# One hybrid decoder layer on one core: the first x tile in one transfer, the first weight split between pairs of x blocks, more idle matmuls at the start

## The chip, the core and the metric

The kernel runs on one core of a Trainium2 chip. The core has a matrix engine (PE), a vector engine (DVE), a scalar engine (ACT), a general engine (POOL), a queue engine that issues transfers (SP), and 16 DMA engines that move data between the device memory and the on-chip memory. The engines run side by side, each through its own list of instructions in order, and wait for one another through semaphores. The metric is the device time of one execution in microseconds (us); lower is better. One execution was also taken with the hardware profiler, and all the rows below come from it.

## What is computed

A decoder layer on 256 positions of width 1024, all in float32. Cut to what matters:

```python
h = rms_norm(x, norm_mix_pre)                 # x: (256, 1024)
proj = h @ w_in                               # w_in: (1024, 9232)
qa, ka, va, qd, kd, vd, zd, bd, ad, ga, gd = split(proj)
ya = moba_attention(rope(qa), rope(ka), va)   # block-sparse attention, 8 heads
yd = gated_deltanet(qd, kd, vd, zd, bd, ad)   # conv, chunked delta rule, gated norm
merged = sigmoid(ga) * (ya @ w_o_attn) + sigmoid(gd) * (yd @ w_o_delta)
x = x + rms_norm(merged @ w_out, norm_mix_post)
h = rms_norm(x, norm_ffn_pre)
f = (silu(h @ w_gate) * (h @ w_up)) @ w_down  # inner width 2816
out = x + rms_norm(f, norm_ffn_post)
```

The part that the change touches is the very beginning: x is loaded and transposed, scaled by the columns of norm_mix_pre, and multiplied by the first 414 columns of w_in that are needed, those with bd and ad and the first part of the gates.

## The kernel before

Every float32 product is made from three faster ones. Each operand is split into a rounded high half and a low half (the rest), and PE adds high x high, low x high and high x low in one bank of its result memory. So each weight piece goes through three steps: SP loads it as `wr` (four buffers in turn), ACT copies it rounded to `wh`, DVE subtracts to get `wl`. The pieces are numbered in the order of their use. `split_to` does a whole piece at once; `split_halves` (line 441) does one of the first two in two steps of 414 columns. x comes in two tiles of 128 rows, `q_x` in the trace (x0 and x1 in the code). PE transposes a tile in eight blocks of 128 x 128 into banks, two blocks to a bank and four to a call of `x_transpose` (line 504). `x_evac` (line 510) then splits each block: ACT writes the high half `q_hh`, scaled by a column of `col0`, and DVE the low half `q_hl`. It goes through the four blocks in the order 0, 2, 1, 3, from one bank to the other and back. `col0` holds norm_mix_pre in columns: eight rows are loaded as `rows0` and transposed by PE.

`start` (line 1109) is the first unit. It issues idle matmuls on a zero tile (`fill`, with the counts WARM and FILL), the transposes of x0, again idle matmuls, and then `part(i, t)`, the six matmuls of weight piece i with x tile t. In between stand the transposes of x1 and the splits of the pieces wr1, wr2 and wr3. At its end the row scales of x are worked out: two times a sum of squares on ACT, a power on POOL and a diagonal `d_dg` on DVE, which PE multiplies by ones. From then on every unit has the same form: load, split, multiply.

`K` is a table of constants that SP loads after the first four weight pieces and some small rows. `mask16` (a cast of a part of K on DVE) and `triur` (a copy of a part of it on ACT) are needed only much later. Their lines stand in another function, `gates`; where they end up in the lists of DVE and ACT is decided when the program is built, by a scheduler that goes by its own estimates. SP issues a transfer only when the completion counter that it is to use is free again; there are eight in turn. So SP issues K when the second x tile has landed, the transfer that had the counter before.

Helpers record every operation, so the trace gives one line for many: 132 is the wrapper of ACT, DVE, POOL and SP, 290 a matmul, 294 a transpose and 1121 an idle matmul. Buffer numbers are left out in the trace.

Of the kernel before, what the change touches and what calls it, by code (L numbers as in the profile page):

```python
# [27 lines left out]
PSUM = bass.MemoryType.PSUM  # L28
MARGIN = 50
STAG = 0  # L30
WARM = 5
DEC = 6
KEEP = 1
FILL = 3


def shape_constants():
# [215 lines left out]
def build(nc, tc, ctx, A):  # L253
    fl = Flow()
    SP, ACT, DVE, POOL, PE = nc.sync, nc.scalar, nc.vector, nc.gpsimd, nc.tensor
    SP, ACT, DVE, POOL = Engine(SP, "S", fl), Engine(ACT, "A", fl), Engine(DVE, "V", fl), Engine(POOL, "P", fl)
# [24 lines left out]
    def mm(out, l, r, start, stop):  # L281
        n = free_size(r)
        if l.dtype == F32R:
            c = max(109.0, 0.4225 * n)
        elif l.dtype == F32:
            c = max(213.0, 1.667 * n)
        else:
            c = max(29.0, 0.44 * n)
        fl.pe(out, l, r, c)
        issue(lambda: PE.matmul(out, l, r, start=start, stop=stop))  # L290

    def tr(out, in_, idn):
        fl.pe(out, in_, idn, 107.0)
        issue(lambda: PE.transpose(out, in_, idn))  # L294
# [11 lines left out]
    def main_bank():  # L306
        while not banks.ok():
            yield banks.ok
        return banks.get([128, 512], F32, "m")
# [22 lines left out]
    rows0 = cst.tile([8, 128], F32, name="rows0")  # L332
    col0 = cst.tile([128, 8], F32, name="col0")
# [17 lines left out]
    xd, wind = A["x"][0], A["w_in"][0]  # L351
# [61 lines left out]
    def load_to(i):  # L413
        while nl[0] <= min(i, len(P) - 1):
            j = nl[0]
            ap, a, b = P[j]
            t = wraw.tile([128, a, b], F32, name=f"wr{j}", tag="wr")
            if isinstance(ap, list):
                w = b // len(ap)
                for i, part in enumerate(ap):  # L420
                    SP.dma_start(t[:, :, w * i:w * i + w], part)
            else:
                SP.dma_start(t, ap)
            raws[j] = t
            nl[0] += 1
# [15 lines left out]
    def split_halves(j):  # L441
        load_to(j)
        _, a, b = P[j]
        r = raws.pop(j)
        hi = wsp.tile([128, a, b], F32R, name=f"wh{j}", tag="wh")
        lo = wsp.tile([128, a, b], F32R, name=f"wl{j}", tag="wl")
        for i in range(a):
            ACT.activation(hi[:, i], r[:, i], AF.Copy)
            DVE.tensor_tensor(lo[:, i], r[:, i], hi[:, i].bitcast(F32), op=ALU.subtract)
        spl[j] = (hi, lo)  # L450
        ns_[0] += 1
        load_to(j + RAW)
        return hi, lo

    def piece(j, la=LA):
        split_to(j + la)
        return spl[j]

    xt = []
    for t in range(2):  # L460
        xx = s4.get([128, 1024], F32, f"x{t}")
        if t == 0:
            for q in range(2):
                SP.dma_start(xx[:, 512 * q:512 * q + 512], xd[0:128, 512 * q:512 * q + 512])
                if q == 0:
                    SP.dma_start(rows0, A["norm_mix_pre"].rearrange("o (k p) -> (o k) p", p=128))
            load_to(1)
        else:
            SP.dma_start(xx, xd[128:256, :])
        xt.append(xx)  # L470
    load_to(RAW - 1)
    SP.dma_start(rows[0:96], A["conv_w"][0].rearrange("i (b p) -> (i b) p", p=128))
# [16 lines left out]
    def split_out(bank_ap, hi_ap, lo_ap, scale=None):  # L489
        if scale is None:  # L490
            ACT.activation(hi_ap, bank_ap, AF.Copy)
            DVE.tensor_tensor(lo_ap, bank_ap, hi_ap.bitcast(F32), op=ALU.subtract)
        else:
            ACT.activation(hi_ap, bank_ap, AF.Copy, scale=scale)
            DVE.scalar_tensor_tensor(lo_ap, bank_ap, scale, hi_ap.bitcast(F32), op0=ALU.mult, op1=ALU.subtract)

    def act_slots(tag):
        his, los = [], []
        for q in range(2):
            his.append((yield from slot(s4, [128, 4, 256], F32R, f"{tag}h{q}")))  # L500
            los.append((yield from slot(s4, [128, 4, 256], F32R, f"{tag}l{q}")))
        return his, los

    def x_transpose(src, q):
        bs = [(yield from main_bank()), (yield from main_bank())]
        for i in range(4):
            tr(bs[i // 2][:, 128 * (i % 2):128 * (i % 2) + 128], src[:, 512 * q + 128 * i:512 * q + 128 * i + 128], ident)
        return bs

    def x_evac(bs, cols, t, his, los, q):  # L510
        ts = slice(128 * t, 128 * t + 128)
        for i in (0, 2, 1, 3):
            k = 4 * q + i
            split_out(bs[i // 2][:, 128 * (i % 2):128 * (i % 2) + 128], his[q][:, i, ts], los[q][:, i, ts],
                      scale=cols[:, k:k + 1])
        main_put(bs[0])
        main_put(bs[1])

    def transpose_scaled(src, cols, t, his, los, q):
        x_evac((yield from x_transpose(src, q)), cols, t, his, los, q)  # L520
# [11 lines left out]
    def main_put(b):  # L532
        banks.put(b)
# [453 lines left out]
    def two_banks():  # L987
        b0 = yield from main_bank()
        b1 = yield from main_bank()
        return [b0, b1]  # L990
# [116 lines left out]
    hT = []  # L1107

    def start():
        hT.extend((yield from act_slots("h")))  # L1110
        with tc.manual_schedule():
            warm = cst.tile([128, 512], F16, name="warm")
            DVE.memset(warm, 0.0)
            DVE.memset(mhalf, -0.5)
            DVE.memset(ones, 1.0)
            ACT.activation(scr[:, 0:4], mhalf[:, 0:4], AF.Square)
            wb = yield from main_bank()

            def fill(n):
                for i in range(n):  # L1120
                    PE.matmul(wb, warm[:, 0:128], warm, start=True, stop=True)

            fill(WARM)
            tr(wb[:, 0:8], rows0, ident[0:8, 0:8])
            DVE.tensor_copy(col0, wb[:, 0:8])
            ev = []
            for q in range(2):
                ev.append((yield from x_transpose(xt[0], q)))
            fill(FILL)
            main_put(wb)  # L1130
            outs = yield from two_banks()
            x_evac(ev[0], col0, 0, hT[0], hT[1], 0)
            pc = [split_halves(0)]
            x_evac(ev[1], col0, 0, hT[0], hT[1], 1)
            pc.append(split_halves(1))

            def part(i, t):
                hi, lo = pc[i]
                n = hi.shape[2]
                ts = slice(128 * t, 128 * t + 128)  # L1140
                for kk in range(2):
                    k = 2 * i + kk
                    ah, al = hT[0][k // 4][:, k % 4, ts], hT[1][k // 4][:, k % 4, ts]
                    mm(outs[t][:, :n], ah, hi[:, kk, :], k == 0, False)
                    mm(outs[t][:, :n], al, hi[:, kk, :], False, False)
                    mm(outs[t][:, :n], ah, lo[:, kk, :], False, k == 7)

            part(0, 0)
            e0 = yield from x_transpose(xt[1], 0)
            part(1, 0)  # L1150
            e1 = yield from x_transpose(xt[1], 1)
            x_evac(e0, col0, 1, hT[0], hT[1], 0)
            pc.append(piece(2, 0))
            x_evac(e1, col0, 1, hT[0], hT[1], 1)
            part(0, 1)
            part(1, 1)
            nrs = {}
            for i in range(2):
                pc.append(piece(3, 0)) if i == 0 else None
                part(2 + i, 0)  # L1160
                part(2 + i, 1)
            for t in range(2):
                ss, rs[t], nrs[t] = small(1), small(1), small(1)
                sq = yield from slot(s4, [128, 1024], F32, "sq")
                ACT.activation(sq, xt[t], AF.Square, accum_out=ss)
                s4.put(sq)
                rs_from(ss, 1.0 / D, rs[t])
                DVE.tensor_scalar(nrs[t], rs[t], -1.0, None, op0=ALU.mult)
                split_to(4 + t)
            ACT.activation(ex, abc, AF.Exp)  # L1170
            b = yield from main_bank()
            tr(b[:, 0:105], rows[0:105, :], ident[0:105, 0:105])
            DVE.tensor_copy(colp[:, 0:105], b[:, 0:105])
            main_put(b)
            held.append(DVE.tensor_copy(id16, ident).ins)
        s4.put(xt[0], xt[1])
        for t in range(2):
            ACT.activation(beta[:, 8 * t:8 * t + 8], outs[t][:, 0:8], AF.Exp, scale=nrs[t])
            DVE.scalar_tensor_tensor(tt[:, 8 * t:8 * t + 8], outs[t][:, 8:16], rs[t], dtb, op0=ALU.mult, op1=ALU.add)
        yield from gate_evac(0, outs)  # L1180
        fl.add("gates", gates())
        yield from spread([rs[0], rs[1]], rsb)
# [207 lines left out]
```

## Time and profile before

| | us |
|---|---|
| median of 3 runs | 549.88 (549.68 to 550.12) |
| the profiled execution | 549.29 |
| its span, first to last instruction | 547.6 |
| PE busy | 534.8 (98%) |
| DVE busy | 368.1 (67%) |
| ACT busy | 315.0 (58%) |
| the 16 DMA engines, share of the span | 53% |

The profiled execution has 1.7 us outside its span. A busy PE tells little about how fast it goes: its clock is granted at one of two levels, 1.2 or 2.4 GHz, and the view of stretches gives the mean of it as a share (1.00 is 2.4 GHz). The chain of waits is followed back from the last instruction: at each step to what released it. A transfer in it stands from its issue to its landing. In the timeline a row joins instructions of one kind that follow each other, and the bracket at its end tells how long the engine stood idle before it and what released it.

### The profile page before, as it was taken

To read this page: it belongs to the slowest core of one execution; us is meant where nothing else is said; L and a number is where in the kernel's file an instruction comes from. 1 tells how busy PE (TensorE), PEld (TensorE's weight loads), DVE (VectorE), ACT (ScalarE), POOL (GpSimd) and SP (SyncE) were. 2 spreads that over 40 slices of the span, in tenths; PEclk is the share of its full clock that TensorE was granted. 3 is DMA by queue.
4 is the path that set the end of the run, shared out by engine and by line. 5 is a ranking of instruction groups with operands and counts; after the bars stand their busy time and mean duration, and the time that the engine had idled before them with its cause. 6 is when DMAs were issued, how large, how long until landed. Compare 5 with 4: busy or idle time off the path is not lost.

```text
span 547.6 us, 8378 instructions
## 1 busy us (share of the span) xinstructions
PE 534.8 (98%) x3156; PEld 460.6 (84%) x3156; DVE 368.1 (67%) x650; ACT 315.0 (58%) x553; POOL 26.4 (5%) x38
## 2 busy tenths in 40 slices
PE   7999999899999999999999999999999999999995
PEld 5988898898989888899889988778888888888884
DVE  4899876895879787866577567586465554554434
ACT  6868658487654965786526544585444544443331
POOL 0000002200000230000000000010000000000000
PEclk8999999999999999999999999999999999999998
DMA  8947765245455252244465766257666665555612
GB/s 258 255 149 216 218 197 150 78 117 167 129 168 158 78 167 64 63 148 155 131 201 187 247 210 195 77 158 259 202 189 193 180 197 176 181 189 192 193 38 78
DMA packets 63035, 90.40 MB, mean 165 GB/s; under 512 B 3233, under 2 KB 35090, under 8 KB 62994
## 3 DMA queue, kind: packets, MB, share of 16 engines
q1 hardware_dynamic: 62994, 89.86, 53.4%
q8 instruction: 25, 0.41, 0.3%
q14 instruction: 16, 0.13, 0.1%
HBM read 88.80 MB, written 1.05 MB: 164 GB/s over the span
## 4 chain that ended last, share of the span: by engine, by line
PE 85%; DVE 4%; ACT 3%; DMA 3%; issue 2%; POOL 2%; SPq 0%; POOLq 0%; DVEq 0%; ACTq 0%
PE b_m L290 73%; PE b_s L290 8%; PE b_s L294 2%; PE b_m L294 2%; DMA q_x<-in_x 1%; DVE wl L132 1%; POOL tiny L132 1%; DMA K<-in_shape_k 1%; DMA wr<-in_w_in 1%; ACT wh L132 1%; ACT L132 0%; DVE h_a L132 0%; DVE q_vT L132 0%; SPq L132 0%; ACT d_js L132 0%
## 5 line engine op out<-in xcount | busy, mean ns | idle before, releaser
L132 DVE TENSOR_TENSOR wl<-wr,wh 128x1024 fp32r<-128x1024 f32 (+3 forms) x168 | 197.8, 1184 | 120.8 <-ACT wh L132 116.9
L132 ACT ACTIVATE wh<-wr 128x1024 fp32r<-128x1024 f32 (+3 forms) x168 | 171.8, 1030 | 151.6 <-PE b_m L290 142.9
L290 PE MATMUL b_m<-wh,q_fh 128*128 128x512 f32 x264 | 103.5, 392 | 0.5 <-DVE q_fl L132 0.5
L290 PE MATMUL b_m<-wl,q_fh 128*128 128x512 f32 x264 | 103.0, 390 | 0.0
L290 PE MATMUL b_m<-wh,q_fl 128*128 128x512 f32 x264 | 102.7, 390 | 0.0
L290 PE MATMUL b_m<-wh,q_hh 128*128 128x512 f32 (+2 forms) x208 | 83.1, 400 | 1.0 <-ACT wh L132 1.0
L290 PE MATMUL b_m<-wl,q_hh 128*128 128x512 f32 (+2 forms) x208 | 78.8, 379 | 0.0
L290 PE MATMUL b_m<-wh,q_hl 128*128 128x512 f32 (+2 forms) x208 | 78.8, 379 | 0.0
L290 PEld LDWEIGHTS b_m<-wh,q_fh 128*128 128x128 f32 x264 | 49.6, 188 | 11.0 <-DVE q_fl L132 1.0
L290 PEld LDWEIGHTS b_m<-wl,q_fh 128*128 128x128 f32 x264 | 49.6, 188 | 10.7 <-DVE wl L132 0.7
L290 PEld LDWEIGHTS b_m<-wh,q_fl 128*128 128x128 f32 x264 | 49.5, 188 | 10.3
L290 PE MATMUL b_m<-q_hh,wh 128*128 128x256 f32 x192 | 56.3, 293 | 0.0
L290 PE MATMUL b_m<-q_hl,wh 128*128 128x256 f32 x192 | 54.4, 283 | 0.0
L290 PE MATMUL b_m<-q_hh,wl 128*128 128x256 f32 x192 | 54.4, 283 | 0.0
L290 PEld LDWEIGHTS b_m<-wh,q_hh 128*128 128x128 f32 x208 | 39.5, 190 | 5.4 <-ACT wh L132 1.5
L290 PEld LDWEIGHTS b_m<-wh,q_hl 128*128 128x128 f32 x208 | 39.5, 190 | 5.3
L290 PEld LDWEIGHTS b_m<-wl,q_hh 128*128 128x128 f32 x208 | 39.6, 190 | 4.3 <-DVE wl L132 0.5
L132 POOL TENSOR_TENSOR tiny<-tiny,mhalf 128x4 f32<-128x4 f32 (+1 forms) x20 | 17.4, 873 | 471.3 <-DVE tiny L132 471.3
L290 PEld LDWEIGHTS b_m<-q_hh,wh 128*128 128x128 f32 x192 | 36.7, 191 | 0.4
L290 PEld LDWEIGHTS b_m<-q_hl,wh 128*128 128x128 f32 x192 | 36.7, 191 | 0.3
L290 PEld LDWEIGHTS b_m<-q_hh,wl 128*128 128x128 f32 x192 | 36.7, 191 | 0.1
L132 ACT ACTIVATE h_U<-b_s 128x256 f16<-128x256 f32 (+1 forms) x28 | 11.5, 415 | 10.9 <-PE b_s L290 10.9
(204 smaller groups left out, 718.0 us busy)
## 6 DMA issues: line engine op xcount, KB each, us to landing
wr<-in_w_in SPq DMA_DIRECT2D x56, 512.0 KB, 3.8
wr<-in_w_down SPq DMA_DIRECT2D x22, 512.0 KB, 3.3
wr<-in_w_gate SPq DMA_DIRECT2D x20, 512.0 KB, 3.7
wr<-in_w_up SPq DMA_DIRECT2D x20, 512.0 KB, 3.7
wr<-in_w_in SPq DMA_DIRECT2D x12, 412.0 KB, 3.4
wr<-in_w_o_attn SPq DMA_DIRECT2D x8, 512.0 KB, 4.4
wr<-in_w_o_delta SPq DMA_DIRECT2D x8, 512.0 KB, 4.2
wr<-in_w_out SPq DMA_DIRECT2D x8, 512.0 KB, 3.7
```

What stands on the lines that cost most here:

```text
L132: r = f(*args, **kw)
L290: issue(lambda: PE.matmul(out, l, r, start=start, stop=stop))
L294: issue(lambda: PE.transpose(out, in_, idn))
```

## The change

Four things, all in the first microseconds of the program:

- x0 is loaded by one transfer of 128 rows of 4 KB instead of two of 2 KB rows, and the small transfer of rows0 is issued by ACT instead of SP.
- WARM goes from 5 to 7, FILL from 3 to 8: more idle matmuls ahead of the transposes of x0 and behind them.
- The four blocks of x0's first half are split in the order 0, 1, 2, 3 in two pairs. Weight piece 0 is split behind the first pair and piece 1 behind the second, then come the four blocks of x0's second half.
- `x_evac` gets its order as an argument and frees its banks when the last block is through.

```diff
-WARM = 5
+WARM = 7
-FILL = 3
+FILL = 8
...
+    ACT.dma_start(rows0, A["norm_mix_pre"].rearrange("o (k p) -> (o k) p", p=128))
     xt = []
     for t in range(2):
         xx = s4.get([128, 1024], F32, f"x{t}")
-        if t == 0:
-            for q in range(2):
-                SP.dma_start(xx[:, 512 * q:512 * q + 512], xd[0:128, 512 * q:512 * q + 512])
-                if q == 0:
-                    SP.dma_start(rows0, A["norm_mix_pre"].rearrange("o (k p) -> (o k) p", p=128))
-            load_to(1)
-        else:
-            SP.dma_start(xx, xd[128:256, :])
+        SP.dma_start(xx, xd[128 * t:128 * t + 128, :])
+        load_to(1)
         xt.append(xx)
...
-    def x_evac(bs, cols, t, his, los, q):
+    def x_evac(bs, cols, t, his, los, q, order=(0, 2, 1, 3)):
...
-        for i in (0, 2, 1, 3):
+        for i in order:
...
-        main_put(bs[0])
-        main_put(bs[1])
+        if order[-1] == 3:
+            main_put(bs[0])
+            main_put(bs[1])
...
-            x_evac(ev[0], col0, 0, hT[0], hT[1], 0)
+            x_evac(ev[0], col0, 0, hT[0], hT[1], 0, (0, 1))
             pc = [split_halves(0)]
+            x_evac(ev[0], col0, 0, hT[0], hT[1], 0, (2, 3))
+            pc.append(split_halves(1))
             x_evac(ev[1], col0, 0, hT[0], hT[1], 1)
-            pc.append(split_halves(1))
```

The lists of DVE and ACT change by more than the lines that were moved. This is DVE's list before, from the first split of x blocks to the split of piece 3 (names carry a number; `wl_169`, `wl_185`, `wl_225` and `wl_251` are pieces 0 to 3, an operation on 128x128 is one block of x):

```order
L132 SCALAR_TENSOR_TENSOR q_hl_125<-b_m,col_78,q_hh_124 128x128 x4
L132 TENSOR_TENSOR wl_169<-wr_102,wh_168 128x414 x2
L132 SCALAR_TENSOR_TENSOR q_hl_127<-b_m,col_78,q_hh_126 128x128 x4
L132 TENSOR_TENSOR wl_185<-wr_104,wh_184 128x414 x2
L132 SCALAR_TENSOR_TENSOR q_hl_125<-b_m,col_78,q_hh_124 128x128 x4
L132 CAST mask_76<-K 128x128
L132 TENSOR_TENSOR wl_225<-wr_108,wh_224 128x828
L132 SCALAR_TENSOR_TENSOR q_hl_127<-b_m,col_78,q_hh_126 128x128 x4
L132 TENSOR_TENSOR wl_251<-wr_110,wh_250 128x828
```

And DVE's list after, for the same stretch (`wl_171`, `wl_183`, `wl_231` and `wl_257` are pieces 0 to 3):

```order
L132 SCALAR_TENSOR_TENSOR q_hl_124<-b_m,col_78,q_hh_123 128x128 x2
L132 TENSOR_TENSOR wl_171<-wr_101,wh_170 128x414 x2
L132 SCALAR_TENSOR_TENSOR q_hl_124<-b_m,col_78,q_hh_123 128x128 x2
L132 TENSOR_TENSOR wl_183<-wr_103,wh_182 128x414 x2
L132 SCALAR_TENSOR_TENSOR q_hl_126<-b_m,col_78,q_hh_125 128x128 x4
L132 SCALAR_TENSOR_TENSOR q_hl_124<-b_m,col_78,q_hh_123 128x128 x2
L132 CAST mask_76<-K 128x128
L132 SCALAR_TENSOR_TENSOR q_hl_124<-b_m,col_78,q_hh_123 128x128 x2
L132 TENSOR_TENSOR wl_231<-wr_107,wh_230 128x828
L132 SCALAR_TENSOR_TENSOR q_hl_126<-b_m,col_78,q_hh_125 128x128 x4
L132 TENSOR_TENSOR wl_257<-wr_109,wh_256 128x828
```

One pair of x0's blocks has moved behind piece 0, and the cast of the mask has moved ahead of the last pair of x1's first four blocks. On ACT the list before, from the conversion of piece 1 to that of piece 3 (`wh_184`, `wh_224`, `wh_250`):

```order
L132 ACTIVATE wh_184<-wr_104 128x414 x2
L132 ACTIVATE q_hh_124<-b_m,col_78 128x128 x4
L132 ACTIVATE wh_224<-wr_108 128x828
L132 ACTIVATE q_hh_126<-b_m,col_78 128x128 x2
L132 ACTIVATE triur<-K 128x128
L132 ACTIVATE q_hh_126<-b_m,col_78 128x128 x2
L132 ACTIVATE wh_250<-wr_110 128x828
```

And on ACT after, for the same stretch (`wh_182`, `wh_230`, `wh_256`):

```order
L132 ACTIVATE wh_182<-wr_103 128x414 x2
L132 ACTIVATE q_hh_125<-b_m,col_78 128x128 x4
L132 ACTIVATE q_hh_123<-b_m,col_78 128x128 x2
L132 ACTIVATE triur<-K 128x128
L132 ACTIVATE q_hh_123<-b_m,col_78 128x128 x2
L132 ACTIVATE wh_230<-wr_107 128x828
L132 ACTIVATE q_hh_125<-b_m,col_78 128x128 x4
L132 ACTIVATE wh_256<-wr_109 128x828
```

`triur` has moved ahead of two of x1's first blocks, of the conversion of piece 2 and of two of x1's last blocks.

## Rows read from the trace of the kernel before

**Rows 1.** The page: busy time of PE, share of the span, instructions.

```profile
PE 534.8 (98%) x3156; PEld 460.6 (84%) x3156; DVE 368.1 (67%) x650; ACT 315.0 (58%) x553; POOL 26.4 (5%) x38
```

**Rows 2.** The chain of waits, 0 to 40 us: start us, us, what.

```profile
3.05 6.79 DMA q_x<-in_x
...
9.86 3.99 DMA K<-in_shape_k
...
13.87 0.04 DVE mask L132
...
14.01 1.01 DVE wl L132
...
16.76 1.02 DVE wl L132
...
17.80 0.16 DVE tiny L132
...
21.24 13.89 PE b_m L290 x102
```

**Rows 3.** DMA engines, 0 to 16 us in 40 slices: busy tenths, GB/s.

```profile
DMA  0000378689779999999999999999999697999999
GB/s 0 0 0 0 61 271 302 138 255 210 151 188 265 166 240 327 377 421 415 437 392 400 387 391 393 380 276 290 346 378 380 216 157 165 229 297 276 283 329 347
```

**Rows 4.** Timeline of SP: start us, us, engine line operation out<-in count [idle before].

```profile
1.25 0.36 SPq L132 DMA_DIRECT2D rows<-in_norm_mix_pre  x1
...
2.06 0.94 SPq L132 DMA_DIRECT2D wr<-in_w_in  x2
...
9.86 0.33 SPq L132 DMA_DIRECT2D K<-in_shape_k  x1
```

**Rows 5.** Timeline of DVE, 0 to 24 us.

```profile
8.01 1.09 DVE L132 TENSOR_TENSOR wl<-wr,wh 128x414 fp32r<-128x414 f32 x2 [1.62 <-ACT wh L132]
...
10.49 1.09 DVE L132 TENSOR_TENSOR wl<-wr,wh 128x414 fp32r<-128x414 f32 x2
11.50 0.60 DVE L132 SCALAR_TENSOR_TENSOR q_hl<-b_m,col,q_hh 128x128 fp32r<-128x128 f32 x2
12.28 0.61 DVE L132 SCALAR_TENSOR_TENSOR q_hl<-b_m,col,q_hh 128x128 fp32r<-128x128 f32 x2 [0.18 <-ACT q_hh L132]
```

**Rows 6.** Timeline of ACT, 0 to 24 us.

```profile
7.43 0.99 ACT L132 ACTIVATE wh<-wr 128x414 fp32r<-128x414 f32 x2 [1.42 <-DMA wr<-in_w_in]
...
9.39 0.62 ACT L132 ACTIVATE q_hh<-b_m,col 128x128 fp32r<-128x128 f32 x2 [0.47 <-DVE q_hl L132]
9.92 0.97 ACT L132 ACTIVATE wh<-wr 128x414 fp32r<-128x414 f32 x2
...
12.40 0.89 ACT L132 ACTIVATE wh<-wr 128x828 fp32r<-128x828 f32 x1
...
13.87 0.31 ACT L132 ACTIVATE triur<-K 128x128 fp32r<-128x128 f32 x1
```

**Rows 7.** Timeline of PE, 0 to 24 us.

```profile
1.25 2.31 PE L1121 MATMUL b_m<-warm 128*128 128x512 f16 x5 [1.25 <-DVE mhalf L132]
...
5.71 0.66 PE L294 MATMUL b_m<-ident,q_x 128*128 128x128 f32 x4 [0.89 <-DMA q_x<-in_x]
6.21 0.81 PE L1121 MATMUL b_m<-warm 128*128 128x512 f16 x3
8.03 0.62 PE L290 MATMUL b_m<-wh,q_hh 128*128 128x414 f32 x1 [1.01 <-ACT wh L132]
...
21.24 0.70 PE L290 MATMUL b_m<-d_dg,ones 128*128 128x256 f32 x2 [0.22 <-DVE d_dg L132]
```

**Rows 8.** Stretches: us, busy time (and count) by engine, PE clock, DMA share, GB/s.

```profile
8.03:9.90 1.87, 1.87 (x6) 1.59 (x7) 1.70 (x5) 1.40 (x5) 0.00 (x0) 0.53 1.03 396
9.90:11.40 1.50, 1.50 (x8) 1.36 (x7) 1.41 (x4) 1.44 (x5) 0.00 (x0) 0.50 1.05 308
...
14.00:17.80 3.80, 3.80 (x21) 3.55 (x19) 3.18 (x7) 2.66 (x7) 0.00 (x0) 1.00 1.07 304
```

## The prediction

> **What bounds the kernel now.** I read the page first: PE is busy for 98% of the span [rows 1], so time is won or lost only where PE starts late or stands still. Then the chain of waits over the first 40 us [rows 2], because the change touches nothing behind it: apart from names, the instructions of every engine stand in the same order in both kernels from the split of wr3 on. The reader is to see there that the chain is not on PE until 21.24. It runs over the load of the second x tile, the load of the constants K (issued at 9.86, landed 3.99 later, 13.85), the cast of the mask that waits for it, the splits of weight pieces wr2 (14.01) and wr3 (16.76 to 17.78), the two row-scale chains (from 17.80), and only then 102 matmuls of PE in a row. PE itself waits 0.22 us at 21.24 for DVE's d_dg [rows 7]: from 8 to 21 us PE and the pair ACT/DVE run nearly level, with ACT/DVE last. From 21.24 PE is the chain. So what the change does to the time is how much earlier or later the matmul of 21.24 can start; that shift goes through to the end, since what follows is PE work, or waits for work that starts equally later.
>
> **The change part by part.**
>
> *Transfers.* SP issues x's first tile as one transfer instead of two, and rows0 goes to ACT's queue, so wr0 is issued right behind x, where the second issue stood: at about 1.25 instead of 2.06, 0.8 us earlier [rows 4]. It helps only as far as the DMA engines had room. They show it: from 2.0 to 4.8 us the slices read 7, 8, 6, 8, 9, 7, 7 tenths, from 4.8 on 9 [rows 3]. The gaps add up to 0.4 x (0.3+0.2+0.4+0.2+0.1+0.3+0.3) = 0.7 us, somewhat less since the digits are rounded down. The bytes are the same. I call s the time by which everything behind x lands earlier, and take 0.6. Lower bound 0: the gaps stay, or one engine's queue was full anyway and the last of its packets sets the landing. Upper bound 1.6: the slices from 2.8 to 6.0 carry only 138 to 265 GB/s, about 200 on average, where those from 6.4 on carry 377 to 437 [rows 3]; if that slow stretch of 3.2 us came from the split of x, the same bytes would take 1.6 us. I lean to the gaps, because the slow stretch goes on after x's second half was read at 5.71 [rows 7]. K is issued, before and after, when the second x tile has landed (its completion counter is used again), so K moves with s too: to 13.85 - 0.6 = 13.25.
>
> *x in one piece, seven warm fills.* Two more fills at 2.31 / 5 = 0.46 us each [rows 7] put the transposes, and so the first block of x on ACT, 0.9 us later. Before, ACT was through with four blocks and then waited 1.42 us for wr0 at 7.43 [rows 6]; that wait, and two blocks instead of four, cover the 0.9. It would cost only if s went beyond about 1.
>
> *Weight split behind two blocks.* Before, four blocks of the first quarter were split while wr0 was on its way, for nothing. Now two of them stand behind wr0's split, on both engines. On DVE the way from ACT's start on wr0 (7.43) to the cast was 0.58 to wl0 (8.01), 2.48 to wl1 (10.49), 1.01 to the next pair (11.50), 0.6 for it and 0.8 for the pair at 12.28 [rows 5, 6]. In the new order it is wl0, pair, wl1, four blocks, pair, cast. The moved pair reads one bank, and in this kernel ACT's second block of a bank starts only when DVE is through with the first (ACT stood 0.47 us at 9.39 for that [rows 6]); so it takes about 0.35 + 0.4 + 0.35 us, not 0.6. Summed: 0.58 + 2.48 + 1.01 + 0.6 + about 1.0 = 5.7 us from ACT's start on wr0, so DVE is at the cast at 6.83 + 5.7 = 12.5. K lands at 13.25. The extra work is hidden by the wait for K, with 0.7 us left, and this holds for every s, since both ends move with it. It comes on the path only if K lands more than 0.7 us earlier than wr0's shift makes it.
>
> *What now stands behind K.* This is the term that counts, and the diff doesn't show it; the order does. Cast and triur wait for K, and they have moved up by one pair on DVE and by wr2's conversion and two blocks on ACT. Before, ACT converted wr2 at 12.40 to 13.29, before K was there [rows 6], and DVE could split it at 14.01, 0.16 after K's landing [rows 2]. Now behind K come, on ACT: triur (0.31), a pair of blocks (0.62, as at 9.39), wr2's conversion (0.89), each starting some 0.1 before the one ahead of it ends, as wr1's did at 9.92 behind the pair [rows 6]; that puts the conversion at +0.79 to +1.68, and DVE splits wr2 at +1.70. PE's matmuls with the second x tile wait for the pair, those with wr2 for the split. That is 1.54 later behind K. From there the pattern is the old one: 2.75 us from wr2's split to wr3's (14.01 to 16.76), 1.04 to the row scales (17.80), 3.44 to PE's matmul at 21.24 [rows 2]; the same instructions in the same order. Bounds of this term: 1.2, if the pair behind K overlaps better; 1.9, if it waits block by block. I take 1.54, which is from rows of just these instructions.
>
> *Eight fills.* Three before, eight now, at 0.81 / 3 = 0.27 us [rows 7]: 8 x 0.27 = 2.2 us. The transposes, at 5.71 before for x's second half, are all through by then or a little earlier, so the fills end near 7.7 at most, and wr0's first half is ready at about 7.4 (8.03 - 0.6). A delay of PE of 0.3 at most. They cover the 1.01 us in which PE waited before the first matmul [rows 7]. After that wait the granted clock was 0.53 and 0.50 from 8.03 to 11.40, the lower level, 1.2 GHz [rows 8]; kept at 2.4 GHz the stretch of 3.37 us would need half, 1.7 us. I count this at nothing: PE gets through earlier and then waits for the pair of blocks behind K. Its work that is left then, 33 matmuls of this unit at 3.80 / 21 = 0.18 us [rows 8], is 6 us beside the 8.3 that ACT and DVE take from there to the d_dg matmul, and waits for wr2 and wr3 in between.
>
> The Trainium skill, page "TensorE: Matmul & The Clock Gate", section "What's actually happening", says that "the default state is throttled, and activity releases the throttle". By that rule alone the fills give the stretch its full clock, and the sum would be a gain; the rows agree on the clock, but the chain of waits says that it isn't PE that ends last there.
>
> *Sum.* +1.54 behind K, -0.6 from the earlier landing: the matmul of 21.24 starts at 22.18, 0.94 us later. The profiled execution took 549.29 (span 547.6 and 1.7 around it), so 550.2 by its own measure; the median of the runs, 549.88, lies 0.59 above it, and with it I predict 549.88 + 0.94 = 550.8. A measurement of this kernel can tell about 0.2%, 1.1 us, from no change: the forecast is inside, near its slow end.
>
> **The rivals.**
>
> *Slower: the transfers don't move.* If the last packet of wr0 and of x's second tile comes from an engine whose queue was full from 3.5 us on, s is 0 to 0.4 and the 1.54 stays nearly whole: 551.0 to 551.4. It decides at s = 0.44. For it: from 4.8 us on the digits show no room [rows 3]. Against: the visible gaps ahead of that. A second fall of the clock, while PE stands before the blocks behind K, would add up to 0.5 us: 551.9 at most. 0.33 together.
>
> *No change, lower: the slow stretch goes.* If one transfer of x ends the stretch at 200 GB/s, s is 1.0 to 1.6, K lands at 12.3 to 12.9, and the sum is +0.5 to -0.1: 549.8 to 550.4. For it: the low rate begins with x's second half. Against: it outlasts it. 0.16.
>
> *Faster: PE ends last after all.* If ACT and DVE had more slack than the chain says, the clock kept up gives up to 1.7 us: 548.2. For it: PE had no idle to speak of from 8.03 to 11.40 and from 14.0 to 17.8 [rows 8]. Against: the wait at 21.24, and the pair behind K. 0.10.
>
> That the fills don't bridge the wait (the load later than they last) is a case without a price of its own: the forecast's time.
>
> **How the numbers follow.** Forecast, s from 0.44 to 1.0, 550.4 to 551.0: 0.41. Slower 0.33, the earlier load 0.16, PE last 0.10. Faster by over 0.2% is then 0.10, within it 0.41 + 0.16 = 0.57, slower 0.33. The range runs from 549.5 (the earliest load, less a few tenths of spread: the runs before lie 0.4 apart) to 551.8, and leaves out the faster case and the end of the slow one.
>
> **What would show it.** In the profile of the changed kernel: wr issued at about 1.25; K landed at 13.0 to 13.5; the cast of the mask behind an idle of some tenths on DVE; wr2's conversion on ACT behind triur, not before it; the split of wr2 1.7 us behind K's landing; the d_dg matmul near 22.2 with a wait of PE in front of it; granted clock 1.00 from 8 to 11 us without the end coming nearer. I am wrong if the chain of waits runs over PE between 8 and 21 us, or if K lands before 12.7 or after 13.7.

## The result, and the profile after

The changed kernel takes 552.68 us (median of 4 runs, 552.30 to 552.77) beside 549.78 for the kernel before on the same chip: a ratio of 1.0052, 95% interval 1.0039 to 1.0064, so 2.9 us (2.1 to 3.5) slower. The span of the profiled execution grew from 547.6 to 551.0 us. The forecast was 550.8 and its range ended at 551.8; the time lies 0.9 above it.

PE's share of the span hardly moved; it has seven matmuls more than in [rows 1]. On the page:

```profile
PE 536.1 (97%) x3163; PEld 460.8 (84%) x3163; DVE 368.3 (67%) x650; ACT 314.5 (57%) x553; POOL 26.4 (5%) x38
```

The chain of waits of the changed kernel, 0 to 47 us (start us, us, what), answers to [rows 2]:

```profile
2.21 6.50 DMA q_x<-in_x
8.73 5.69 DMA K<-in_shape_k
...
14.44 0.31 ACT triur L132
14.75 0.51 ACT q_hh L132 x2
15.26 0.79 ACT wh L132
...
16.08 1.02 DVE wl L132
...
18.84 1.02 DVE wl L132
...
23.31 13.89 PE b_m L290 x102
...
40.54 5.14 DMA wr<-in_w_in
...
45.76 0.04 ACT wh L132
```

Two losses can be read off it. The first: the d_dg matmul starts at 23.31 instead of 21.24, 2.07 later. From K's landing to it, it is now 8.89 us (14.42 to 23.31) instead of 7.39 (13.85 to 21.24), because triur, a pair of blocks and wr2's conversion stand ahead of wr2's split; and K itself landed 0.57 later in this execution. The second I had not looked for: at 40.54 the chain passes over a weight transfer of 5.14 us. The same transfer stands in the chain of the kernel before too, but there it took 3.68:

```profile
38.48 3.68 DMA wr<-in_w_in
```

That is 1.46 us more, and 2.07 + 1.46 = 3.5 is the whole growth of the span (3.4). PE's own starts say the same: counted from the end of the program, a matmul at 49 us starts 2.05 later than in the kernel before, one at 55 us 3.52 later, and the last one 3.49.

The stretches of the changed kernel (us, busy time and count by engine PE, PEld, DVE, ACT, POOL, PE clock, DMA share, GB/s) and the first real matmul of PE, beside [rows 7, 8]; and the first instructions of DVE and ACT behind K:

```profile
8.03:9.90 1.87, 1.87 (x12) 1.67 (x11) 1.35 (x4) 1.61 (x5) 0.00 (x0) 1.00 1.05 390
9.90:11.40 1.50, 1.50 (x12) 1.44 (x11) 1.32 (x5) 1.03 (x5) 0.00 (x0) 1.00 1.12 316
11.40:14.00 2.60, 1.07 (x7) 0.57 (x5) 0.64 (x3) 0.25 (x1) 0.00 (x0) 1.00 0.92 236
```

```profile
8.28 0.54 PE L290 MATMUL b_m<-wh,q_hh 128*128 128x414 f32 x1
...
15.06 0.46 PE L290 MATMUL b_m<-wh,q_hh 128*128 128x414 f32 x1 [2.59 <-ACT q_hh L132]
```

```profile
14.44 0.23 DVE L132 CAST mask<-K 128x128 f16<-128x128 f32 x1 [2.40 <-DMA K<-in_shape_k]
```

```profile
14.44 0.31 ACT L132 ACTIVATE triur<-K 128x128 fp32r<-128x128 f32 x1 [2.79 <-DMA K<-in_shape_k]
14.66 0.61 ACT L132 ACTIVATE q_hh<-b_m,col 128x128 fp32r<-128x128 f32 x2
15.16 0.89 ACT L132 ACTIVATE wh<-wr 128x828 fp32r<-128x828 f32 x1
```

The clock reads 1.00 where it read 0.53 and 0.50, and PE does 24 matmuls from 8.03 to 11.40 instead of 14 (transposes and idle ones counted). Nothing comes of it: all three engines then stand before K or what waits for it, ACT for 2.79 us, DVE for 2.40, PE for 2.59.

### The profile page after: what moved, and what is told of

It is laid out like the page before. It is cut to its first block, busy times and chain, and to the rows that moved or that the text cites. A ratio compares the mean times of both kernels' runs of the same rounds, so it can differ in the third digit from the quotient of the medians.

```text
span 551.0 us, 8390 instructions
## 1 busy us (share of the span) xinstructions
PE 536.1 (97%) x3163; PEld 460.8 (84%) x3163; DVE 368.3 (67%) x650; ACT 314.5 (57%) x553; POOL 26.4 (5%) x38
## 4 chain that ended last, share of the span: by engine, by line
PE 85%; DVE 4%; DMA 3%; ACT 3%; issue 2%; POOL 2%; SPq 0%; POOLq 0%; DVEq 0%; ACTq 0%
PE b_m L290 73%; PE b_s L290 8%; PE b_s L294 2%; PE b_m L294 1%; DVE wl L132 1%; DMA q_x<-in_x 1%; POOL tiny L132 1%; DMA K<-in_shape_k 1%; DMA wr<-in_w_in 1%; ACT wh L132 1%; DVE h_a L132 0%; DVE q_vT L132 0%; ACT d_js L132 0%; DVE tiny L132 0%; DVE h_T L132 0%
```

## Why a weight transfer far behind the start became slower

The DMA view of the stretch around that transfer tells it: busy tenths and GB/s in 40 slices, then the queues (packets, MB, share). First before (38.4 to 43.6 us), then after (40.5 to 45.7):

```profile
GB/s 0 0 0 0 0 0 0 0 24 118 110 110 138 217 335 331 343 347 347 351 347 347 335 284 158 106 197 264 280 311 280 284 315 347 347 343 296 213 142 99
q1 hardware_dynamic: 2076, 1.05, 71.0%
```

```profile
GB/s 0 0 0 0 0 0 0 0 150 79 91 87 189 303 307 335 311 339 323 343 323 339 327 288 205 134 173 291 315 311 319 343 319 335 339 307 272 118 59 55
...
q8 instruction: 1, 0.02, 1.6%
issues: line engine op xcount, KB each, median us to landing
wr<-in_w_in SPq DMA_DIRECT2D x2, 512.0 KB, 5.1
```

After, a packet of the queue "q8 instruction" lies in the stretch, 16 KB at 41.62: its 1.6% of 16 engines over 5.2 us is 1.3 us of one engine (1.34 in the trace). Before, the same kind of packet comes at 43.64, 1.5 us after the transfer has landed (42.16). The page counts 25 of them over the whole execution, in both kernels. I read them as loads of PE's program text, because this one moves with the number of PE's instructions (the table below): counted from the start of the chain's 102 matmuls it comes at 21.9 to 22.7 us in the seven kernels without extra ones (22.40 before), at 18.3 to 19.3 with seven more matmuls (after, e1, e4), at 11.5 to 14.8 with 30 or 37 (e9 to e11). The change gives PE 14 more instructions (seven weight loads, seven matmuls), and that brings this load forward to 18.31. **Theory A**: the second loss is this meeting of a load of program text with a transfer that is on the chain; the first is what stands behind K. **Rivals**: the fills or the late K slow the transfer in some other way; the fills' own time costs; the order would not matter with the old transfers; all the loss goes once K is out of the way.

## Experiments

The ratios are to the kernel before on the same chip, with 95% intervals. "K to d_dg" is from K's landing to the start of the chain's 102 matmuls, "program text" the start of the packet near the weight transfer, "transfer" what that transfer takes; "off" marks what the chain view does not pass over. "Lost" is how much more PE lags behind the kernel before at 55 us than at 49 us, by the starts of the same matmuls.

| kernel | ratio | median us | d_dg | K to d_dg | program text | transfer | lost |
|---|---|---|---|---|---|---|---|
| before | 1 | 549.8 | 21.24 | 7.39 | 43.64 | 3.68 | 0 |
| after | 1.0052 [1.0039, 1.0064] | 552.68 | 23.31 | 8.89 | 41.62 | 5.14 | 1.47 |
| e1 before, 7 tiny matmuls | 1.0026 [1.0015, 1.0036] | 551.28 | 20.73 | 7.39 | 40.02 | 5.18 | 1.50 |
| e2 before, new fills | 1.0138 [1.0123, 1.0154] | 557.62 | 21.78 | 7.39, off | 39.47 | 3.60, off | other order |
| e3 after, old fills | 1.0010 [1.0000, 1.0020] | 550.56 | 22.43 | 8.90 | 44.32 | 3.67 | -0.01 |
| e4 after, late cast | 0.9992 [0.9984, 1.0001] | 549.47 | 21.11 | off | 40.27 | 4.94 | 0.78 |
| e5 after, late cast, old fills | 0.9965 [0.9952, 0.9977] | 548.17 | 20.55 | off | 42.91 | 3.75, off | -0.04 |
| e6 before, late cast | 0.9977 [0.9967, 0.9987] | 548.78 | 20.32 | off | 42.50 | 3.67, off | -0.04 |
| e7 x in one transfer only | 1.0007 [0.9996, 1.0018] | 550.52 | 21.99 | 8.63 | 44.11 | 3.72 | 0.05 |
| e8 order only | 1.0018 [1.0008, 1.0028] | 551.23 | 22.82 | 8.63 | 44.82 | 3.86 | 0.18 |
| e9 before, 30 tiny matmuls | 1.0003 [0.9992, 1.0014] | 550.07 | 22.70 | 7.39, off | 37.51 | 3.80 | 0.12 |
| e10 after, 30 tiny matmuls | 1.0014 [1.0005, 1.0023] | 550.38 | 22.66 | 8.64 | 34.26 | 3.77 | 0.11 |
| e11 e4, 30 tiny matmuls | 0.9985 [0.9976, 0.9994] | 548.95 | 21.26 | off | 32.77 | 3.79, off | -0.06 |
| e12 x in one transfer, late cast | 0.9961 [0.9949, 0.9974] | 547.62 | 19.57 | off | 42.22 | 3.80, off | -0.05 |

**e1: only more instructions on PE.** The kernel before, with seven idle matmuls of two columns:

```diff
             fill(WARM)
+            for i in range(7):
+                PE.matmul(wb[:, 0:2], warm[:, 0:128], warm[:, 0:2], start=True, stop=True)
```

> The kernel before with seven extra idle matmuls of 2 columns (14 more instructions on PE, hardly any work) behind its five warm ones; nothing else moves. Theory A: the changed kernel lost in two places, 2.1 us at the constants K (cast and triur moved up, K landed 0.6 us late) and 1.5 us at the weight transfer issued at 40.5 (it took 5.14 us, against 3.68 before at 38.5), the second because 14 more PE instructions bring a load of PE's program text, 16 KB on one DMA engine, forward into that transfer. Then this kernel lands that transfer about 1.5 us later than before, and takes 549.8 + 1.4 = 551.2. Rival B: the second loss is a consequence of the first shift or of chance in the DMA engines; then this kernel takes 549.8, within 0.3.

The ratio is 1.0026, 1.4 us slower, though the d_dg matmul came earlier here (20.73) than before. Its chain, and the DMA view from 37.9 to 43.1 us:

```profile
37.96 5.18 DMA wr<-in_w_in
```

```profile
GB/s 0 0 0 0 0 0 0 0 35 98 165 189 240 295 307 343 461 323 335 315 335 311 280 205 154 173 295 311 315 256 343 343 351 339 351 288 158 67 24 24
...
q8 instruction: 1, 0.02, 1.1%
```

At its end the transfer moves 24 GB/s, a fourteenth of its 340: as when one DMA engine of the 16 still works. The trace shows it in the completion counter too. It gets 16 signals for each such transfer, as many as there are DMA engines. After, 15 of them come 3.27 to 3.66 us behind the issue and the last at 5.14; in e1 15 by 3.58 and the last at 5.18; in e4 15 by 3.53 and the last at 4.94. In the eleven other kernels all 16 are there by 3.60 to 3.86. Theory A holds so far.

**e9 and e10: still more instructions, less time.** If the place of the load is what counts, enough extra instructions must carry it past the transfer. The same line with 30 instead of 7, in the kernel before (e9) and in the changed one (e10):

```diff
+            for i in range(30):
+                PE.matmul(wb[:, 0:2], warm[:, 0:128], warm[:, 0:2], start=True, stop=True)
```

> The kernel before with 30 idle matmuls of 2 columns behind the warm fills (e1 had 7); the other engines' instructions stand as before. Theory A (what cost e1 its 1.4 us was the place of the load of PE's program text, not the extra instructions): 60 instructions bring the load forward so far that it comes ahead of the weight transfer, at 35 to 37.5 us, the transfer issued near 38.5 takes 3.6 to 3.9 us again, and the time is that of the kernel before, 549.8 (549.3 to 550.4): more extra instructions, less time. Rival (extra instructions or matmuls cost by themselves, or make the weight transfer late in some other way): 551.3 or more, transfer 4.9 to 5.2.

> The changed kernel with 30 idle matmuls of 2 columns behind its warm fills. Theory A: the load of program text comes ahead of the weight transfer (36 to 39 us), the transfer issued near 40.5 takes 3.6 to 3.9 us instead of 5.14, and of the two losses only the one behind K is left: 552.7 - 1.5 = 551.2 (550.7 to 551.8). Rival (the late transfer has another cause in the changed kernel): 552.7 or, with the 30 matmuls' own time, up to 553.2.

Both as theory A had it: 1.0003 and 1.0014. From the chain of e9, then of e10:

```profile
39.94 3.80 DMA wr<-in_w_in
```

```profile
39.88 3.77 DMA wr<-in_w_in
```

The program text was loaded at 37.51 and 34.26, before these transfers were issued. With 0, 7 and 30 extra matmuls the kernel before takes 549.8, 551.28 and 550.07. A cost for each instruction, or for its time, cannot do that; the place of the load goes with it in the table. e9's d_dg is late in its profiled execution (22.70) because K landed late there, at 15.31; it comes 7.39 behind K, as before. (e10's 550.38 is below the 550.7 to 551.8 expected; in this kernel the order on ACT has one more block ahead of triur, and K to d_dg is 8.64, not 8.89.)

**e3: the changed kernel with the old fills.**

```diff
-WARM = 7
+WARM = 5
-FILL = 8
+FILL = 3
```

> The changed kernel with the old counts of idle matmuls, 5 and 3. Theory A: the loss at K stays, 1.5 to 2.1 us by how late K lands, the loss at the later transfer goes: 551.3 to 551.9. Rival B: 552.7, as changed.

The loss of 2.9 us falls to 0.6 (0 to 1.1), further than expected: 550.56 is 0.7 under theory A's 551.3. In its profiled execution K landed at 13.53, 0.9 earlier than in the changed kernel, and d_dg came 1.19 later than before, not 2.07. The chain has K to d_dg as long as after, and the transfer short again:

```profile
8.59 4.94 DMA K<-in_shape_k
...
22.43 13.89 PE b_m L290 x102
...
39.65 3.67 DMA wr<-in_w_in
```

So 8.89 and 8.90 behind K don't depend on the fills.

**e2: the kernel before with the new fills.** This was meant to be the fills alone:

```diff
-WARM = 5
+WARM = 7
-FILL = 3
+FILL = 8
```

> Before with only the counts of idle matmuls changed, 7 and 8. Theory A: the lists of ACT and DVE are those of before, so nothing is lost at K; the 14 more PE instructions cost the 1.5 us at the later transfer: 551.2, and the granted clock is 1.00 from 8 to 11 us without a gain. Rival B: 549.8. Rival C, that PE sets the end of the first 20 us: 1.7 us gained, 548.1.

It is 7.7 us slower (1.0138), and as a test of the fills it failed. With the new counts the scheduler wrote the lists of DVE, ACT and PE in another order far behind the start, between 27 and 57 us, where the edit touches nothing. The chain waits at 41.45 for a POOL instruction of 5.98 us, which takes 0.64 to 0.94 in the other chains; then PE's clock is at half, the lower level, from 45.8 to 52.7:

```profile
41.45 5.98 POOL d_dc L132
```

```profile
45.80:52.70 6.90, 5.23 (x15) 4.27 (x16) 1.11 (x1) 2.94 (x3) 1.61 (x1) 0.51 0.55 184
```

What made POOL slow in that order was not tried. The load of program text at 39.47 costs e2's transfer (issued at 36.61) nothing: it comes when that is moving its last packets. In the other kernels of the table these lists differ from those of the kernel before only at the start, where the edits are, but for the five with the late cast (e4 to e6, e11, e12): there triur and the cast stand where the edit puts them, and one copy of ACT, `d_dT`, comes some 4 us earlier (41.61 in e5, 45.68 before), where the edit touches nothing.

**e8 and e7: the order alone, the transfer alone.** e8 takes over only the new order of the blocks; e7 only x in one piece and rows0 on ACT's queue.

```diff
-            x_evac(ev[0], col0, 0, hT[0], hT[1], 0)
+            x_evac(ev[0], col0, 0, hT[0], hT[1], 0, (0, 1))
...
-            x_evac(ev[1], col0, 0, hT[0], hT[1], 1)
+            x_evac(ev[0], col0, 0, hT[0], hT[1], 0, (2, 3))
...
+            x_evac(ev[1], col0, 0, hT[0], hT[1], 1)
```

> The kernel before with only the new order of the blocks (the weight's split behind two of them); transfers and fills as before. Theory A (the loss at the start is the order: a pair of blocks and wr2's conversion stand behind K): K's landing to d_dg 8.4 to 8.9 instead of 7.4, and 551.0 (550.6 to 551.4), with the program text loaded after 43 us. Rival (the loss needs the changed transfers too: with the old ones K is late enough that the order doesn't matter): 549.8 (549.4 to 550.2).

```diff
+    ACT.dma_start(rows0, A["norm_mix_pre"].rearrange("o (k p) -> (o k) p", p=128))
...
-            for q in range(2):
-                SP.dma_start(xx[:, 512 * q:512 * q + 512], xd[0:128, 512 * q:512 * q + 512])
...
+        SP.dma_start(xx, xd[128 * t:128 * t + 128, :])
+        load_to(1)
```

> The kernel before with only x's first tile in one transfer and rows0 on ACT's queue; order of the pairs and fills as before. PE has no extra instruction. In this kernel's order the cast stands between the two blocks of a pair on DVE and triur ahead of the last of four blocks on ACT, so that some of the work stands behind K here too. Theory A (K lands no earlier with x in one piece: 13.4 to 14.4; what stands behind it is longer than before by 0.6 to 1.2): 550.6 (550.2 to 551.0), K's landing to d_dg 8.0 to 8.6, program text loaded after 43 us. Rival (the transfer moves everything earlier by s = 0.6, as predicted): K at 13.25, and 549.8 (549.4 to 550.1).

The order alone costs 1.0 us (0.4 to 1.5); K to d_dg is 8.63. The transfer alone, in whose list the cast and triur moved forward as well, has the same 8.63 and costs 0.4 (-0.2 to 1.0). That is between theory A's 0.8 and its rival's nothing, so e7's time does not decide between them; its rows have both, K landed early (13.36) and more behind it. The chains of e8 and e7:

```profile
10.22 3.97 DMA K<-in_shape_k
...
22.82 13.89 PE b_m L290 x102
```

```profile
8.43 4.93 DMA K<-in_shape_k
...
21.99 13.89 PE b_m L290 x102
```

**e4 to e6, e11, e12: K out of the way.** triur and the mask are needed only behind the row scales. The same edit in e4 (changed kernel), e5 (changed kernel, old fills), e6 (kernel before) and e12 (kernel before with e7's edit) puts them there:

```diff
-        ACT.activation(triur, triu, AF.Copy)
-        DVE.tensor_copy(mask16, maskT1)
+        with tc.issue_after(held[1]):
+            ACT.activation(triur, triu, AF.Copy)
+        with tc.issue_after(held[0]):
+            DVE.tensor_copy(mask16, maskT1)
...
-            ACT.activation(ex, abc, AF.Exp)
+            hx = ACT.activation(ex, abc, AF.Exp)
...
+            held.append(hx.ins)
```

> The changed kernel with triur and the mask's cast put behind the first unit (triur behind the exponential of a_log, the cast behind id16), so that nothing waits for K early. Theory A: the loss at K goes and turns into a gain, since DVE needs not wait: the d_dg matmul at about 20.5 instead of 23.3 (21.24 before); with the later transfer still hit, 549.8 - 0.7 + 1.4 = 550.5, and 549.1 if it is not. Rival D, that the loss is in the pairs of blocks or in the clock and not in the wait for K: 552.7.

> The changed kernel with triur and the mask's cast put behind later work, as in e4, and with the old number of fills (5 warm, 3 per pair). Theory A (two losses, each for itself: the work that stands behind K's landing, and PE's 14 extra instructions, which bring the load of its program text forward into a weight transfer): neither loss is left, the load of program text comes after 43 us, the weight transfer issued near 38 to 39.5 takes 3.6 to 3.9 us, and the time is e4's 549.5 less 1.5, so 548.0 (547.6 to 548.6), faster than both kernels. Theory B (e4 gained from the late cast all that there is, and fills and program text don't matter once the cast is late): 549.5 (549.1 to 549.9). Theory C (without the fills the clock falls again between 8 and 11 us, and with nothing waiting for K now PE is what ends last there): d_dg 1 to 1.7 us later than with fills, 549.5 to 550.2 even with the transfer at 3.7.

> The kernel before with only triur and the mask's cast put behind later work; transfers, order of the pairs and fills as before. Theory A (K's landing was the last wait of the start, by 0.2 to 0.8 us over the way through wr0 and wr1): 549.1 (548.8 to 549.6), the d_dg matmul at 20.5 to 21.0 and the chain of waits no longer over K. Rival (ACT and DVE, not K, end last anyway): 549.8, d_dg at 21.1 to 21.4.

> The kernel before with x's first tile in one transfer (rows0 on ACT's queue) and triur and the mask's cast late; order of the pairs and fills as before. Against e6 it is the transfer alone, with no wait for K to hide it. If the earlier wr0 (landed about 0.65 earlier with x in one piece) is worth its time once K is out of the way: 548.2 (547.7 to 548.6), d_dg 0.3 to 0.7 earlier than e6's 20.32. Rival (a later weight piece sets the end instead, and lands no earlier): 548.8 (548.5 to 549.3), d_dg at 20.2 to 20.6.

e4 loses the first loss and keeps the second, in part: its transfer takes 4.94, but PE loses only 0.78 there. Its time is 1.0 below the 550.5 expected for a transfer that is still hit: that costs less here than the 1.4 counted. In its profiled execution d_dg came at 21.11, later than the 20.5 expected. e5 loses both and is faster than both kernels, 548.17, as theory A had it to 0.2 us. e6 gains 1.3 us (0.7 to 1.8), more than the 0.7 expected; its d_dg is at 20.32, 0.92 earlier than before. e12, at 547.62, is the fastest: x in one transfer brings d_dg from 20.32 to 19.57 once nothing waits for K. It is just under the 547.7 to 548.6 expected, and its interval overlaps those of e5 and e6. Chains of e5, e6 and e12 in turn:

```profile
20.55 13.88 PE b_m L290 x102
```

```profile
20.32 13.88 PE b_m L290 x102
```

```profile
19.57 13.89 PE b_m L290 x102
```

e11 is e4 with the 30 tiny matmuls:

> The kernel of e4 (the changed kernel with triur and the mask's cast put late, all its fills) with 30 idle matmuls of 2 columns behind the warm fills. Theory A (program text ahead of the transfer; the clock kept up between 8 and 11 us is worth nothing, since ACT and DVE end last there even without the wait for K): 548.2 as e5 (547.7 to 548.7), the granted clock 1.00 from 8 to 11 us, d_dg at 20.5 to 21.1. Rival 1 (with the wait for K gone PE's clock matters): d_dg under 20.2 and 547.0 to 547.6. Rival 2 (the load of program text is not what cost e4 its time against e5): 549.5.

Its 548.95 lies between A's 548.2 and Rival 2's 549.5, and its interval overlaps e4's, so the time alone does not decide between these two; Rival 1 is out, d_dg is at 21.26. At the weight transfer the rows are as A has it: with the program text loaded at 32.77 the transfer takes 3.79, and PE loses nothing there, where e4 lost 0.78. The chain says where the 0.7 above A come from: without K to wait for, it starts on PE, over the warm fills and the tiny matmuls themselves, up to the transposes:

```profile
1.25 3.17 PE b_m L1119 x7
4.42 0.78 PE b_m L1123 x30
```

From the first split of a weight on (DVE's wl at 7.68, in e5 at 6.96) the way to d_dg is 13.58, in e5 13.59; the 0.7 lies ahead of it. I had counted the 30 as hidden, as they are in e10 behind K.

## Why the prediction was wrong

**Right: what stands behind K.** 1.54 was forecast, 8.89 - 7.39 = 1.50 measured; the split of wr2 came 1.66 us behind K's landing (1.70 forecast), with ACT's three instructions in the forecast order, and e8 shows that the order alone does most of it (8.63, 1.24 more). **Right: the fills are no gain.** The clock came up and the chain did not notice; the wait at 15.06 in front of PE is the one forecast. The page "TensorE: Matmul & The Clock Gate" of the Trainium skill, section "What's actually happening", by which activity releases a clock that is throttled by default, fits the changed kernel's 1.00. The view of stretches reads 1.00 from 8 to 11.4 us in e3 and e6 too, which have the old fills, but there it says nothing: the trace's first record of the clock begins at 9.70 and 10.18 in these two, and a time without a record counts as 1.00. PE's rows decide. Two matmuls of 414 columns each, from the kernel before, from e3 and from the changed kernel:

```profile
8.44 0.55 PE L290 MATMUL b_m<-wh,q_hl 128*128 128x414 f32 x1
8.79 0.58 PE L290 MATMUL b_m<-wl,q_hh 128*128 128x414 f32 x1
```

```profile
7.87 0.55 PE L290 MATMUL b_m<-wh,q_hl 128*128 128x414 f32 x1
8.22 0.55 PE L290 MATMUL b_m<-wl,q_hh 128*128 128x414 f32 x1
```

```profile
8.65 0.34 PE L290 MATMUL b_m<-wh,q_hl 128*128 128x414 f32 x1
8.84 0.35 PE L290 MATMUL b_m<-wl,q_hh 128*128 128x414 f32 x1
```

In e3 they start 0.35 apart, as in the kernel before at its lower level (0.53 and 0.50 [rows 8]); in the changed kernel 0.19. All five kernels with the new fills have some 0.19 there, and of the nine with the old fills only e12. So the new fills bring the clock up ahead of these matmuls, and it is worth nothing: with K out of the way d_dg is at 20.55 with the old fills and the 0.35 (e5), and at 21.11 and 21.26 with the new ones and the 0.19 (e4, e11). The fills ended later than the 7.7 forecast, the first real matmul started at 8.28, and the wait for K hid that too. **Right: the moved pair is hidden**; DVE was through by 12.04 (12.5 forecast).

**The landing, right on average and wrong in the profiled execution.** wr was issued at 1.23 as forecast and K at 8.73, 1.13 earlier, but K landed at 14.42, not 13.25, outside the 12.7 to 13.7 that I had set as a sign of being wrong. The profiled d_dg matmul came 2.07 later and not 0.94; this landing is the whole difference. From issue to landing K takes anything from 3.97 to 5.73 us with the transfers of before (six profiles) and from 3.93 to 5.69 with x in one piece (eight). So the landings scatter: between 13.34 (e1) and 15.31 (e9), both with the transfers of before. On average over these profiles x in one piece has K issued 0.81 earlier (8.88 beside 9.69) and landed 0.51 earlier (13.77 beside 14.28), with single landings 0.4 to 0.7 around their mean. One trace says little about such a term. The medians say more: with the new order in both, x in one piece brings e3 0.4 us below e8 (by the ratios), though its way behind K is 0.3 longer; with K out of the way, e12 is 0.9 below e6. Both are about the 0.6 forecast, within their intervals. Without the program text the sum +0.94 holds: e3 is at +0.6 (0 to 1.1) and e10 at +0.8 (0.3 to 1.3).

**Wrong: "eight fills: 0", and the premise that the change touches nothing behind the start.** I priced the fills by their time on PE and asked what covers it. What they cost was not time but place: 14 more instructions put a load of program text into the weight transfer at 40 us, and that transfer, 3.68 us before, was on the chain. The term that is missing in the sum is 1.46 by the rows and 1.4 by e1; the changed kernel against e10 and e3 gives 2.1 to 2.3. e4 against e5 (0.9992 to 0.9965) gives 1.5, but in the profiled executions 0.56 of that lies ahead of d_dg (21.11 and 20.55). Part of it was there to be read: the page of the kernel before lists the 25 packets, the trace has one 1.5 us behind the landing of a transfer that the chain runs over. How far seven matmuls move it was not. None of the rivals had it either.

**Open.** The 0.7 us by which 2.1 to 2.3 exceeds 1.46 is not settled: K's late landing would account for it if it was late in all four runs of the changed kernel, and only one was profiled. In the profiled executions d_dg is 0.88 earlier in e3 and 0.65 in e10, and e10 gains 0.44 more between 95 and 108 us, as e8 and e9 do; why is open. Which DMA engine carried the 16 KB packet the trace does not name. That it is the one whose signal comes last is argued, from the 15 others that are in time and from the kernels in which the load falls elsewhere.

## What to carry to other kernels

Count the instructions that stand behind the last input to land, on each engine, and move what isn't needed yet behind the path: that was worth 0.2% in the kernel before (e6), more than any part of the change as written. An instruction that costs no time still has a place in its engine's program: when a change adds some, look in the DMA view for the loads of program text, and at which transfer of the chain they will meet; and check that a scheduler didn't rewrite lists that the edit doesn't touch, as in e2. Take the landing of a transfer from several executions or from medians before building a sum of tenths on it.

## What was not expected of the hardware

- A load of 16 KB of PE's program text within a 512 KB weight transfer makes it land after 4.94 to 5.18 us (after, e1, e4) instead of 3.60 to 3.86 (the eleven others). 15 of the transfer's 16 signals come in time, the last 1.4 to 1.6 us behind them; the packet itself takes 0.93 to 1.34 on its engine.
- The load moved by more than the added instructions take: counted from the start of the 102 matmuls, from 22.40 us (before) to 19.29 with seven more matmuls (e1) and 14.81 with thirty (e9), though the thirty take only 0.78 us on PE (e11).
- K, the same transfer in the same place of the program, took 3.93 to 5.73 us from issue to landing in the fourteen profiles, with x in one piece as with x in two.
